# An expert-parallel MoE layer on one core: one late output store and weights in plain order

## The chip, the core and the metric

The kernel runs on one core of one Trainium2 chip. A core has a matrix engine (TensorE, in the profile PE, with its weight loads as PEld), VectorE (DVE), ScalarE (ACT), GpSimd (POOL) and SyncE (SP), an on-chip memory (SBUF) of 128 partitions, and a smaller accumulator memory (PSUM) into which TensorE writes. Sixteen DMA engines move data between the chip's main memory (HBM) and SBUF. They work through queues that SyncE and GpSimd fill. The metric is the device time of one execution in microseconds, as the median of several runs.

## What is computed

Eight experts, each a two-layer network with a ReLU between, on its own 256 rows of input:

```python
n_experts, capacity, hidden, expert_hidden = 8, 256, 512, 2048
x:  (8, 256, 512)    w1: (8, 512, 2048)    w2: (8, 2048, 512)    # all float32

h = np.matmul(x, w1)
h = np.maximum(h, 0)
return np.matmul(h, w2).astype(np.float32)
```

Each w1 and each w2 of an expert is 4 MB in float32, each x and each output 0.5 MB. All of it passes through HBM once: 64 MB of weights, 4 MB of x and 4 MB of output.

## The kernel before

**Loads.** The weights are cast from float32 to bf16 by the DMA itself, so on chip an expert's w1 and w2 are 2 MB each. `load_w1` (line 82) brings a w1 in one DMA. `load_w2` (line 88) brings a w2 in as many DMAs as the table `PIECES` says, counted in sixteenths: one for experts 0 to 5, two halves for expert 6, a half and two quarters for expert 7. `load_x` (line 74) brings the x of two experts at once. All of these are issued by GpSimd, on one queue, and are carried out in the order of issue. The x of experts 0 and 1 alone come through SyncE (line 67) and are cast by VectorE (line 69).

**Order.** The list `loads` holds the loads by expert: x of a pair where one is due, w1, w2. The line `loads[-3], loads[-2] = loads[-2], loads[-3]` exchanges two of them, so that w1 of expert 7 comes ahead of w2 of expert 6. `issue` takes loads from the front of the list as long as they are in the set that it is given, so the main loop says how far ahead loads are issued. There are four buffers for w1 and four for w2; a load waits on GpSimd until the expert that used its buffer has been computed. The order of TensorE's and GpSimd's instructions is the order of the program (`manual_schedule`).

**Compute of one expert.** `prepare` transposes x on TensorE (line 119, 8 transposes) and copies it back to SBUF on VectorE (line 121). `layer1` does 64 matmuls with pieces of w1 as the stationary operand (line 135), and after each 8 of them ScalarE applies the ReLU and writes bf16 (line 142). `layer2` does 32 matmuls (line 161) into two PSUM tiles, one for each half of the 256 rows. Where w2 comes in pieces, both tiles advance together through the pieces; else one tile is finished first. The finished tiles are copied to an output tile in SBUF on VectorE (line 172), the very last one on ScalarE (line 170).

**Main loop.** For each expert from 0 to 6: issue loads, layer 1 of this expert, x of the next one, layer 2 of this expert. In the round of expert 6, layer 1 of expert 7 stands between: TensorE does layer 1 of 6, layer 1 of 7, layer 2 of 6, layer 2 of 7, as the weights arrive in this order.

**Stores.** `GROUPS` sets which outputs share an SBUF tile and a store. Experts 0, 1 and 2 are stored together (1.5 MB, line 92), issued in the round of expert 3; in GpSimd's queue this store stands behind w1 of expert 7 and ahead of w2 of expert 6. Experts 3 to 6 (2 MB, line 92) are stored after everything else on GpSimd. Expert 7's output (0.5 MB, line 174) is stored by SyncE.

The identity matrix for the transposes is built on GpSimd (`make_identity`, a memset and a select), once behind the first and once behind the second weight load.

Of the kernel before, what the change touches and what calls it, by code (L numbers as in the profile page):

```python
# [14 lines left out]
def kernel(  # L15
# [7 lines left out]
    nc = tc.nc  # L23
    P = 128
    E, C, H = x.shape
# [26 lines left out]
    identity = const.tile([P, P], BF16, name="identity")  # L52


    PIECES = {E - 2: [8, 8], E - 1: [8, 4, 4]}


    GROUPS = [(0, 1, 2), (3, 4, 5, 6), (7,)]
    GROUP = {e: g for g in GROUPS for e in g}
    DEFER = GROUPS[-2]  # L60
    X_GROUPS = [(2, 3), (4, 5), (6, 7)]

    xbs, w1s, w2s, outs = {}, {}, {}, {}
# [20 lines left out]
    def load_w2(e):  # L84
        w2s[e] = t = w2_pool.tile([P, K2 * H], BF16, name="w2_sb")
        k = 0
        for n in PIECES.get(e, [K2]):
            nc.gpsimd.dma_start(t[:, k * H:(k + n) * H], w2_v[e, :, k * H:(k + n) * H])  # L88
            k += n

    def store(g):
        nc.gpsimd.dma_start(  # L92
            og_v[:, g[0]:g[-1] + 1, :], outs[g][:].rearrange("p e m h -> p e (m h)")
        )

    loads = []
    for e in range(E):
        for g in X_GROUPS:  # L100
            if g[0] == e + 1:
                loads.append((load_x, g))
        loads += [(load_w1, e), (load_w2, e)]
    loads[-3], loads[-2] = loads[-2], loads[-3]

    def issue(upto):
        while loads:
            f, e = loads[0]
            if (f, e) not in upto:
                break  # L110
            loads.pop(0)
            f(e)

    def prepare(e):
        xb = xbs[e]
        xt_ps = psum_t.tile([P, K1, MC, P], BF16, name="xt_ps")
        for ko in range(K1):
            for mo in range(MC):
                nc.tensor.transpose(xt_ps[:, ko, mo, :], xb[:, mo, :, ko], identity[:])  # L119
        xT = xT_pool.tile([P, K1, C], BF16, name="xT")  # L120
        nc.vector.tensor_copy(  # L121
            xT[:].rearrange("p k c -> p (k c)"),
            xt_ps[:].rearrange("p k m q -> p (k m q)"),
        )
        return xT

    def layer1(e, xT):
        w1_r = w1s[e][:].rearrange("p (ko q j) -> p ko q j", ko=K1, j=K2)
        hT = hT_pool.tile([P, K2, C], BF16, name="hT")
        for pr in range(K2 // 2):  # L130
            h_ps = psum_h.tile([P, 2, C], FP32, name="h_ps")
            for s in range(2):
                j = pr * 2 + s
                for ko in range(K1):
                    nc.tensor.matmul(  # L135
                        h_ps[:, s, :],
                        w1_r[:, ko, :, j],
                        xT[:, ko, :],
                        start=(ko == 0),
                        stop=(ko == K1 - 1),  # L140
                    )
            nc.scalar.activation(  # L142
                hT[:, pr * 2:pr * 2 + 2, :].rearrange("p a c -> p (a c)"),
                h_ps[:].rearrange("p a c -> p (a c)"),
                mybir.ActivationFunctionType.Relu,
            )
        return hT

    def layer2(e, hT):
        last = e == E - 1  # L150
        g = GROUP[e]
        if e == g[0]:
            outs[g] = out_pool.tile([P, len(g), MC, H], FP32, name=f"out_sb{g[0]}")
        out_sb = outs[g][:, e - g[0]]
        o_ps = [psum_o.tile([P, H], FP32, name="o_ps") for _ in range(MC)]
        if e in PIECES:
            order = [(k, m) for k in range(K2) for m in range(MC)]
        else:
            order = [(k, m) for m in range(MC) for k in range(K2)]
        for k, m in order:  # L160
            nc.tensor.matmul(  # L161
                o_ps[m][:],
                hT[:, k, m * P:(m + 1) * P],
                w2s[e][:, k * H:(k + 1) * H],
                start=(k == 0),
                stop=(k == K2 - 1),
            )
            if k == K2 - 1:
                if last and m == 1:
                    nc.scalar.copy(out_sb[:, m, :], o_ps[m][:])  # L170
                else:
                    nc.vector.tensor_copy(out_sb[:, m, :], o_ps[m][:])  # L172
        if last:
            nc.sync.dma_start(out_v[e], out_sb.rearrange("p m h -> p (m h)"))
# [3 lines left out]
    with tc.manual_schedule(engines={mybir.EngineType.PE, mybir.EngineType.Pool}):  # L178
        f, e = loads.pop(0)
        f(e)  # L180
        make_identity(nc, identity)
        f, e = loads.pop(0)
        f(e)
        make_identity(nc, identity)
        issue([(load_w2, 0), (load_x, X_GROUPS[0]), (load_w1, 1), (load_w2, 1), (load_w1, 2)])
        xT = prepare(0)
        for e in range(E - 1):
            issue(
                [(load_w2, e + 2), (load_w1, e + 3), (load_w1, E - 1), (load_w2, e + 1)]
                + [(load_x, g) for g in X_GROUPS if g[0] <= e + 4]  # L190
            )
            for g in GROUPS[:-2]:
                if g[-1] == e - 1:
                    store(g)
            hT = layer1(e, xT)
            xT = prepare(e + 1)
            if e == E - 2:
                hT_last = layer1(E - 1, xT)
            layer2(e, hT)
        store(DEFER)  # L200
        layer2(E - 1, hT_last)
# [1 line left out]
_INS = ['x', 'w1', 'w2']  # L203
_OUTS = [((8, 256, 512), 'float32')]
# [25 lines left out]
```

## Time and profile before

| What | us |
|---|---|
| median of four runs | 182.53 (182.12 to 182.68) |
| the profiled execution: its own time | 182.68 |
| its span, first to last instruction | 180.9 |
| TensorE busy in matmuls | 127.5 |
| ScalarE busy | 40.1 |
| VectorE busy | 17.1 |
| GpSimd busy | 15.4 |

The span is what the profile's views cover; 1.8 us of the profiled time lie outside it. "Idle before" in a group's line is time in which that engine waited, with what ended the wait behind it. TensorE waited 36.4 us at line 135 for w1 and 6.7 us at line 161 for w2; in the last 12 us it waited for nothing. The DMA issues of the page are these; "us to landing" runs from the issue to the arrival of the last byte, the time in the queue included:

```profile
w_sb<-in_w_dram POOLq DMA_DIRECT2D x14, 2048.0 KB, 61.3
w_sb<-in_w_dram POOLq DMA_DIRECT2D x3, 1024.0 KB, 57.4
out_dram<-out_sb POOLq DMA_DIRECT2D x1, 2048.0 KB, 9.8
xb<-in_x_dram POOLq DMA_DIRECT2D x3, 512.0 KB, 45.5
out_dram<-out_sb POOLq DMA_DIRECT2D x1, 1536.0 KB, 64.7
x_sb<-in_x_dram SPq DMA_DIRECT2D x2, 512.0 KB, 3.7
w_sb<-in_w_dram POOLq DMA_DIRECT2D x2, 512.0 KB, 46.8
out_dram<-out_sb SPq DMA_DIRECT2D x1, 512.0 KB, 3.4
```

The sizes are those of the bytes written: a weight of 2048 KB is 4 MB read.

### The profile page before, as it was taken

How to read it: one execution, taken by the hardware profiler on the slowest of the kernel's cores; microseconds unless marked ns; L12 is line 12 of the kernel's file. 1: busy time of each engine (PE TensorE's matmuls, PEld its weight loads, DVE VectorE, ACT ScalarE, POOL GpSimd, SP SyncE). 2: the span in 40 equal slices, each digit the busy share in tenths (PEclk: the TensorE clock that was granted, in tenths of full speed). 3: DMA queues.
4: the chain of work that ended last, by engine and by line, in shares of the span. 5: the costliest groups of instructions: out<-in, count | busy, mean ns of one | idle time of the engine just before them, and what ended most of it. 6: DMA issues, size and time to landing. Idle time of an engine off the chain costs nothing.

```text
span 180.9 us, 1851 instructions
## 1 busy us (share of the span) xinstructions
PE 127.5 (70%) x824; PEld 90.3 (50%) x832; DVE 17.1 (9%) x25; ACT 40.1 (22%) x66; POOL 15.4 (8%) x32
## 2 busy tenths in 40 slices
PE   0206999059994959449994959539994966997780
PEld 0105964048743944138842954228841966953330
DVE  1300011100111011100111011100111010000210
ACT  2001530014400730005500630004600552520000
POOL 7601011010000031000201002010100000000100
PEclk9999999957999999957999999957999998899998
DMA  6998999899999989998999999899989989999994
GB/s 214 250 221 185 232 232 214 192 232 225 206 206 232 225 177 236 232 214 192 232 232 210 196 203 253 185 228 232 221 188 228 232 199 350 226 208 215 219 401 176
DMA packets 4919, 40.48 MB, mean 224 GB/s; under 512 B 432, under 2 KB 432, under 8 KB 2736
## 3 DMA queue, kind: packets, MB, share of 16 engines
q0 software_dynamic: 4480, 38.80, 97.3%
q1 hardware_dynamic: 432, 1.57, 2.4%
q8 instruction: 6, 0.10, 0.2%
q14 instruction: 1, 0.01, 0.0%
HBM read 71.30 MB, written 4.19 MB: 417 GB/s over the span
## 4 chain that ended last, share of the span: by engine, by line
PE 61%; DMA 19%; another core or an unknown queue 15%; POOL 1%; issue 1%; ACT 0%; POOLq 0%
PE h_ps L135 32%; PE o_ps L161 27%; DMA w_sb<-in_w_dram 19%; PE xt_ps L119 1%; POOL xb L74 0%; POOL w_sb L82 0%; ACT out_sb L170 0%; POOL identity masks.py:199 0%; POOL identity masks.py:197 0%; POOL w_sb L88 0%; POOLq masks.py:199 0%; POOLq L214 0%
## 5 line engine op out<-in xcount | busy, mean ns | idle before, releaser
L135 PE MATMUL h_ps<-xT,w_sb 128*128 128x256 bf16 x512 | 67.5, 300 | 36.4 <-DMA w_sb<-in_w_dram 36.4
L135 PEld LDWEIGHTS <-w_sb 128*128 128x128 bf16 x512 | 61.3, 149 | 44.1 <-DMA w_sb<-in_w_dram 39.8
L142 ACT ACTIVATE hT<-h_ps 128x512 bf16<-128x512 f32 x64 | 38.2, 597 | 119.9 <-PE h_ps L135 119.9
L161 PE MATMUL o_ps<-w_sb,hT 128*128 128x512 bf16 x248 | 56.3, 379 | 7.2 <-DMA w_sb<-in_w_dram 6.7
L161 PEld LDWEIGHTS <-hT 128*128 128x128 bf16 x256 | 25.0, 98 | 36.3 <-issue 7.8
L172 DVE COPY out_sb<-o_ps 128x512 f32<-128x512 f32 x15 | 10.3, 691 | 64.4 <-PE o_ps L161 64.4
L121 DVE COPY xT<-xt_ps 128x1024 bf16<-128x1024 bf16 x8 | 5.5, 690 | 90.4 <-PE xt_ps L119 90.4
L88 POOL DMA_DIRECT2D w_sb<-in_w_dram x11 | 5.9, 536 | 57.9 <-DMA w_sb<-in_w_dram 55.6
L119 PE MATMUL xt_ps<-identity,xb 128*128 128x128 bf16 x64 | 5.3, 230 | 4.8 <-DVE xb L69 4.8
L82 POOL DMA_DIRECT2D w_sb<-in_w_dram x8 | 4.7, 593 | 31.7 <-PE h_ps L135 18.6
L119 PEld LDWEIGHTS <-xb 128*128 128x128 bf16 x64 | 4.7, 117 | 4.8 <-DVE xb L69 4.8
L92 POOL DMA_DIRECT2D out_dram<-out_sb x2 | 1.5, 755 | 38.1 <-DVE out_sb L172 37.9
L74 POOL DMA_DIRECT2D xb<-in_x_dram x3 | 2.1, 716 | 26.4 <-PE xt_ps L119 26.4
L170 ACT COPY out_sb<-o_ps 128x512 f32<-128x512 f32 x1 | 0.6, 585 | 15.9 <-PE o_ps L161 15.9
L69 DVE CAST xb<-x_sb 128x1024 bf16<-128x1024 f32 x2 | 1.4, 694 | 4.6 <-DMA x_sb<-in_x_dram 4.6
L142 ACT ACT_TABLE_LOAD x1 | 1.3, 1283 | 0.7 <-PEq L214 0.7
masks.py:199 POOL TENSOR_SCALAR_AFFINE_SELECT identity<-identity 128x128 bf16<-128x128 bf16 x2 | 0.6, 287 | 0.1
masks.py:197 POOL MEMSET identity<- 128x128 bf16 x2 | 0.4, 223 | 0.0
L214 POOL MEMSET const-float32-0.0<- 128x1 f32 x1 | 0.1, 98 | 0.2 <-issue 0.2
L214 POOL MEMSET const-bfloat16-1.0<- 128x1 bf16 x1 | 0.1, 102 | 0.0
L214 POOL MEMSET const-uint8-127<- 128x1 uint8 x1 | 0.1, 102 | 0.0
L214 POOL MEMSET const-float32-1.0<- 128x1 f32 x1 | 0.1, 98 | 0.0
## 6 DMA issues: line engine op xcount, KB each, us to landing
w_sb<-in_w_dram POOLq DMA_DIRECT2D x14, 2048.0 KB, 61.3
w_sb<-in_w_dram POOLq DMA_DIRECT2D x3, 1024.0 KB, 57.4
out_dram<-out_sb POOLq DMA_DIRECT2D x1, 2048.0 KB, 9.8
xb<-in_x_dram POOLq DMA_DIRECT2D x3, 512.0 KB, 45.5
out_dram<-out_sb POOLq DMA_DIRECT2D x1, 1536.0 KB, 64.7
x_sb<-in_x_dram SPq DMA_DIRECT2D x2, 512.0 KB, 3.7
w_sb<-in_w_dram POOLq DMA_DIRECT2D x2, 512.0 KB, 46.8
out_dram<-out_sb SPq DMA_DIRECT2D x1, 512.0 KB, 3.4
```

The lines of the kernel that those rows point to most:

```text
L69: nc.vector.tensor_copy(b[:].rearrange("p m q k -> p (m q k)"), t[:])
L74: nc.gpsimd.dma_start(t[:].rearrange("p e m q k -> p e (m q k)"), xg_v[:, g[0]:g[0] + 2, :])
L82: nc.gpsimd.dma_start(w1s[e][:], w1_v[e])
L88: nc.gpsimd.dma_start(t[:, k * H:(k + n) * H], w2_v[e, :, k * H:(k + n) * H])
L92: nc.gpsimd.dma_start(og_v[:, g[0]:g[-1] + 1, :], outs[g][:].rearrange("p e m h -> p e (m h)"))
L119: nc.tensor.transpose(xt_ps[:, ko, mo, :], xb[:, mo, :, ko], identity[:])
L121: nc.vector.tensor_copy(xT[:].rearrange("p k c -> p (k c)"), xt_ps[:].rearrange("p k m q -> p (k m q)"),)
L135: nc.tensor.matmul(h_ps[:, s, :], w1_r[:, ko, :, j], xT[:, ko, :], start=(ko == 0), stop=(ko == K1 - 1),)
L142: nc.scalar.activation(hT[:, pr * 2:pr * 2 + 2, :].rearrange("p a c -> p (a c)"), h_ps[:].rearrange("p a c -> p (a c)"), mybir.ActivationF ...
L161: nc.tensor.matmul(o_ps[m][:], hT[:, k, m * P:(m + 1) * P], w2s[e][:, k * H:(k + 1) * H], start=(k == 0), stop=(k == K2 - 1),)
L170: nc.scalar.copy(out_sb[:, m, :], o_ps[m][:])
L172: nc.vector.tensor_copy(out_sb[:, m, :], o_ps[m][:])
```

## The change

- Outputs of experts 0 to 6 share one SBUF tile of 28 KB per partition and go out in one store of 3.5 MB, issued on GpSimd behind all loads and behind layer 2 of expert 6. The store in the middle is gone.
- The exchange in the list of loads is gone: w1 of 6, w2 of 6, w1 of 7, w2 of 7. Layer 1 of expert 7 accordingly stands behind layer 2 of expert 6 on TensorE.
- w2 of expert 6 comes in one DMA, w2 of expert 7 in two halves.
- The identity is built once.

```diff
-    PIECES = {E - 2: [8, 8], E - 1: [8, 4, 4]}
+    PIECES = {E - 1: [8, 8]}
...
-    GROUPS = [(0, 1, 2), (3, 4, 5, 6), (7,)]
+    GROUPS = [tuple(range(E - 1)), (E - 1,)]
     GROUP = {e: g for g in GROUPS for e in g}
-    DEFER = GROUPS[-2]
...
-    loads[-3], loads[-2] = loads[-2], loads[-3]
...
         make_identity(nc, identity)
-        f, e = loads.pop(0)
-        f(e)
-        make_identity(nc, identity)
         issue([(load_w2, 0), (load_x, X_GROUPS[0]), (load_w1, 1), (load_w2, 1), (load_w1, 2)])
         xT = prepare(0)
         for e in range(E - 1):
             issue(
-                [(load_w2, e + 2), (load_w1, e + 3), (load_w1, E - 1), (load_w2, e + 1)]
+                [(load_w2, e + 2), (load_w1, e + 3), (load_w2, e + 1)]
                 + [(load_x, g) for g in X_GROUPS if g[0] <= e + 4]
             )
-            for g in GROUPS[:-2]:
-                if g[-1] == e - 1:
-                    store(g)
             hT = layer1(e, xT)
             xT = prepare(e + 1)
-            if e == E - 2:
-                hT_last = layer1(E - 1, xT)
             layer2(e, hT)
-        store(DEFER)
-        layer2(E - 1, hT_last)
+        store(GROUPS[0])
+        hT = layer1(E - 1, xT)
+        layer2(E - 1, hT)
```

## The prediction

> **What bounds the kernel now.** I read first the 40 slices of the page, then the chain that ended last, then the tail in windows and by its DMA issues. All times below are microseconds of the one profiled execution.
>
> ```profile
> PE 127.5 (70%) x824; PEld 90.3 (50%) x832; DVE 17.1 (9%) x25; ACT 40.1 (22%) x66; POOL 15.4 (8%) x32
> ...
> DMA  6998999899999989998999999899989989999994
> ...
> HBM read 71.30 MB, written 4.19 MB: 417 GB/s over the span
> ```
>
> TensorE is busy 70% of the span, the 16 DMA engines nearly all of it, and only the first and last slices are lower. The kernel is one stream of 75.5 MB, and a change helps to the extent that it takes work or a gap out of that stream. The chain of waits shows when each weight became usable, because TensorE waits for it ("another core or an unknown queue" stands where the landing is not attributed):
>
> ```profile
> 38.00 9.52 PE h_ps L135 x64
> ...
> 57.50 7.21 PE h_ps L135 x64
> ...
> 79.32 9.34 PE h_ps L135 x64
> ...
> 98.73 7.21 PE h_ps L135 x64
> ...
> 120.72 9.13 PE h_ps L135 x64
> ...
> 137.43 2.58 another core or an unknown queue
> 140.00 0.05 issue
> 140.05 7.21 PE h_ps L135 x64
> 147.26 0.45 PE xt_ps L119 x8
> 147.71 2.89 another core or an unknown queue
> 150.59 0.05 issue
> 150.64 8.87 PE h_ps L135 x64
> ...
> 164.03 3.61 PE o_ps L161 x16
> ...
> 168.90 4.26 PE o_ps L161 x19
> ```
>
> These are the starts of layer 1 of experts 1 to 7 and of the two waits in layer 2 at the end (second half of w2 of expert 6, first half of w2 of expert 7). From them come the prices of the stream. Two whole weights take 19.50, 19.41 and 19.33 (57.50-38.00, 98.73-79.32, 140.05-120.72), so one takes 9.71. With an x pair between, 21.82 and 21.99, so x is 2.5. A half weight is 4.87 (168.90-164.03). From w1 of expert 7 (150.64) to the end of w2 of expert 6 (164.03) are 13.39; less two halves, 9.74, the 1.5 MB store in the middle of the stream took 3.65, or 2.43 per MB. One step doesn't fit: w1 of expert 7, directly behind w1 of expert 6, took 10.59, which is 0.88 over the 9.71.
>
> ```profile
> out_dram<-out_sb POOLq DMA_DIRECT2D x1, 2048.0 KB, 9.8
> out_dram<-out_sb SPq DMA_DIRECT2D x1, 512.0 KB, 3.4
> ```
>
> These are the two DMA issues of the last 12 (size, time from issue to landing); the next two lines, from the timeline, give their starts.
>
> ```profile
> 169.05 0.76 POOL L92 DMA_DIRECT2D out_dram<-out_sb  x1 [37.93 <-DVE out_sb L172]
> ...
> 176.62 0.35 SPq L174 DMA_DIRECT2D out_dram<-out_sb  x1
> ```
>
> The tail: the 2 MB store lands at 169.05 + 9.8 = 178.85, expert 7's own store at 176.62 + 3.4 = 180.02, and the span is 180.9, so 0.88 follow the last landing. The last weights land near 168.90 + 4.87 = 173.77. The 2.5 MB of output behind them thus end 6.25 later (2.50 per MB, completion included). That is hardly above the 2.43 of the middle store, so the slowest DMA engine has no real gap in the tail, although TensorE computes until 175.98.
>
> **The change part by part.**
> *Middle store gone, one store of 3.5 MB at the end.* Removed: 3.65 ahead of the last w2. Added: 1.5 MB behind it, 3.65 by the same price. Sum 0, unless writes behind each other cost other than writes among reads: 2.43 to 2.50 per MB gives -0.0 to +0.1. The new store holds seven pieces per partition where the old held three and four; both old prices agree, so I scale by bytes. Its cover: it needs expert 6's output. w2 of expert 6 lands at 140.05 + 9.71 = 149.76, its 32 matmuls take 7.07 (the sixth expert's row, 31 matmuls and one before), the copy 0.69: 157.5, and the issue on GpSimd 0.76 for four experts, so up to 1.3 for seven. It stands in the queue from about 158.8, and the weights end at 169.2: 10 of slack. Were that gone, each microsecond of lateness would be one of idle DMA. Nothing is behind this store on GpSimd.
>
> *Plain order of w1 of 7 and w2 of 6.* The bytes are the same. New landings: w2 of 6 at 149.76, w1 of 7 at 159.47, w2 of 7 at 159.47 + 9.74 = 169.21. On GpSimd the three loads now wait for other buffers, but the last five weight transfers are issued 61.6, 60.2, 57.4, 50.4 and 43.2 before they land, so a few microseconds of issue time lie inside the queue.
>
> *Layer 1 of expert 7 moves behind layer 2 of expert 6 on TensorE.* Idle before it: 159.47 - 156.8 = 2.6. In the chain, gaps of 2.58, 2.54 and 2.58 were followed by a layer 1 of 7.21; gaps of 2.93 and about 5 by 8.87 to 9.34. So 7.21 is likely, 9.52 (the longest row) the other end: it ends at 166.7 to 169.0. Layer 2 of expert 7 then is 32 x 0.222 = 7.1 (7.07 in the rows), and its second half of weights is there at 169.21, before its 17th matmul at 170.2. It ends at 173.8 to 176.1, against 175.98 now. The copy (0.58 and 0.03 around it) puts the SP store at 174.4 to 176.7, against 176.62. The 3.5 MB store has bytes left until 169.21 + 3.5 x 2.43 = 177.7, so the SP store joins a busy stream in either case, and the end is set by the stream.
>
> *Pieces.* w2 of 6 comes in one piece instead of two (9.71 against 9.74), w2 of 7 in two instead of three. The quarters have no wait of their own, because TensorE reads them late; their cost is between 0 and what two 512 KB pieces may lose against one of 1 MB, taken as 0.1 from the same kind of difference (0.03) doubled and rounded up. Together -0.03 to -0.13; I take -0.1.
>
> [...]
>
> *Second identity build gone.* Two pairs of instructions, 0.22 + 0.29, ahead of the third DMA issue. That DMA (the x pair) is queued behind eight megabytes of weights, and the first layer 1 waits for w1 at 15.2: 0.
>
> *Sum.* Last weights 169.21, output 4 MB: the 6.25 of the old tail and 1.5 x 2.43 = 3.65 make 9.90, landing 179.1 against 180.02. Of this 0.9, 0.88 is the odd step of w1 of 7, which the sum leaves out because no bytes explain it. If such a delay recurs somewhere in the stream, the gain is the 0.1 of the pieces. The times speak for that: the profiled execution took 182.68, the four runs lie between 182.12 and 182.68, median 182.53, so delays of this size come and go between runs. I take the 0.1 to 0.2 as what is sure, from the median: 182.35.
>
> The clock deserves one more look. [...] The gap of 2.93 before the layer 1 at 150.64 already cost 8.87 - 7.21 = 1.66 here. [...]
>
> **The rivals.**
> *A, bytes conserved (0.45):* the stream is as full as before and carries the same; 182.35, own range 182.1 to 182.7. For it: the tail's 2.50 per MB next to the middle's 2.43. Against it: the odd step.
> *B, the odd 0.88 belongs to the middle store (0.30):* w1 of 7 is the transfer just ahead of that store, and some DMA engines already write output while others still load (the window from 148 to 150 moved 305 GB/s, where weights alone move some 220). Without mixing the step is 9.71, and the end moves by 0.9: 182.53 - 0.9 = 181.65. Against it: nothing like it shows in the tail, where the 2 MB store follows w2 in the same way.
> *C, TensorE becomes the end (0.20), slower:* expert 7's whole compute now hangs on w1 of 7 at 159.47. If that landing is late by the 0.88 (160.35) and the gap so grown (3.5) halves the clock for a while (9.52), layer 2 ends at 160.35 + 9.52 + 7.12 = 177.0, the SP store is issued at 177.6 and lands 3.4 later at 181.0: span 181.9, 0.98 over the old one, time 182.53 + 0.98 = 183.5. It decides from the point at which the last copies end after 176.6. For it: four of the seven quoted layers 1 ran slow. Against: the three at gaps of 2.6 did not.
> *D, the change starves the queue (0.05):* a load waits on GpSimd for a buffer until the queue runs dry; one dry microsecond makes 183.4. Against it: 43 of lead in the least case.
>
> **How the numbers follow.** This kernel's runs tell apart about 0.2%, 0.37 us. A lies almost wholly within it, a little of it on the faster side; B is faster, C and D slower. Faster 0.34, same 0.44, slower 0.22. The range takes in B, with 0.15 below it, and most of C: 181.5 to 183.3; A alone is 182.1 to 182.7.
>
> **What would show it.** In the profile after: no stretch of pure writes before the last weight; layer 1 of expert 7 near 159.5 and 7.2 long; layer 2 of 7 without a wait in its middle; the large store landing about 8.9 after the last weight, and both stores within 1.5 of each other at the end. B shows if w1 of 7 comes 9.7 after w2 of 6 and the span is near 180. C shows as a layer 1 of 9 and an SP store issued after 176.6 that lands last, well after the large one. I am wrong in kind if the output at the end costs clearly more than 2.5 per MB, or if a gap appears in the stream of weights.

## The result, and the profile after

The changed kernel takes 181.89 us (median of 44 runs, 181.50 to 182.55), the kernel before 182.39 us in the same sessions (66 runs, 181.98 to 183.06). The ratio is 0.9973, 95% interval 0.9968 to 0.9979: half a microsecond faster, small and clear of noise.

The profiled execution took 182.45, span 180.7, so it is one of the slower ones of its kernel. Its page, the share of the DMA engines in 40 slices and the issues with size and time to landing:

```profile
DMA  6998999999999989999999999999999999999994
...
HBM read 71.30 MB, written 4.19 MB: 418 GB/s over the span
...
w_sb<-in_w_dram POOLq DMA_DIRECT2D x15, 2048.0 KB, 62.8
out_dram<-out_sb POOLq DMA_DIRECT2D x1, 3584.0 KB, 20.3
...
out_dram<-out_sb SPq DMA_DIRECT2D x1, 512.0 KB, 5.1
```

The same bytes flow as before, and the stream is still full up to the last slice. The chain of waits of the changed kernel from w1 of expert 6 on:

```profile
140.45 0.05 issue
140.49 8.87 PE h_ps L132 x64
149.37 0.45 PE xt_ps L116 x8
149.81 0.32 another core or an unknown queue
150.13 0.04 issue
150.18 0.38 PE o_ps L158
...
157.24 2.61 another core or an unknown queue
159.86 0.05 issue
159.90 7.21 PE h_ps L132 x64
167.11 0.22 PE o_ps L158
167.33 0.05 issue
167.38 6.65 PE o_ps L158 x30
174.03 0.02 issue
174.06 0.58 ACT out_sb L167
```

w2 of expert 6 is usable at 150.13, 9.68 after w1 of 6 (140.45), and w1 of 7 at 159.86, 9.73 later. The step of 10.59 that the old profile had behind w1 of 6 is gone. A w1 of 7 that comes 9.7 after w2 of 6 is the sign that rival B had named. Layer 2 of expert 7 runs without a wait. In the timeline the large store is issued at 158.27, so it lands at 158.27 + 20.3 = 178.6; SyncE's store is issued at 174.66 and lands at 179.8.

Two windows of the same stretch, the kernel before first, then the changed one (columns: stretch, length, busy time of PE, PEld, DVE, ACT and POOL, clock, DMA share, GB/s). A packet is booked where it starts, so a share well above 1 means long packets, or many that start together:

```profile
146.40:147.30 0.90, 0.90 (x12) 0.90 (x11) 0.00 (x0) 0.60 (x2) 0.00 (x0) 1.00 1.78 291
```

```profile
146.40:147.30 0.90, 0.90 (x11) 0.90 (x10) 0.00 (x0) 0.62 (x2) 0.00 (x0) 1.00 1.19 255
```

In the kernel before, 16 packets in a row were slow here, as many as there are DMA engines: 16 KB packets of 1.44 to 2.05 us, where the usual is 1.23, begun between 146.55 and 147.17. The middle store's first packets began at 148.19. In the changed kernel none between 143 and 155 took over 1.23.

The two spans differ by only 0.2, the medians by 0.5. The trace has 16 landings for each transfer, as many as there are DMA engines. For w1 of 6 the first was at 138.47 in the changed kernel's profile and at 138.51 in the old one, but the last at 140.45 and 140.00: up to here both streams carry the same transfers in the same order, and the changed kernel's profile was 0.45 behind. From there to the last landing (179.81 and 180.04) it took 39.36 against 40.04, 0.68 less. Single profiles of this kernel differ by such lags, and a difference of 0.3% is read from the medians.

### The profile page after: what moved, and what is told of

It is laid out like the page before. It is cut to its first block, busy times and chain, and to the rows that moved or that the text cites. A ratio compares the mean times of both kernels' runs of the same rounds, so it can differ in the third digit from the quotient of the medians.

```text
span 180.7 us, 1844 instructions
## 1 busy us (share of the span) xinstructions
PE 126.4 (70%) x824; PEld 89.5 (50%) x832; DVE 17.3 (10%) x25; ACT 40.1 (22%) x66; POOL 13.3 (7%) x27
## 4 chain that ended last, share of the span: by engine, by line
PE 55%; DMA 24%; another core or an unknown queue 14%; POOL 2%; issue 1%; ACT 0%; POOLq 0%
PE o_ps L158 27%; PE h_ps L132 27%; DMA w_sb<-in_w_dram 24%; PE xt_ps L116 1%; POOL w_sb L81 1%; POOL xb L73 0%; ACT out_sb L167 0%; POOL w_sb L87 0%; POOL identity masks.py:199 0%; POOL identity masks.py:197 0%; POOLq masks.py:199 0%; POOLq L204 0%
## 5 line engine op out<-in xcount | busy, mean ns | idle before, releaser
L132 PE MATMUL h_ps<-xT,w_sb 128*128 128x256 bf16 x512 | 66.3, 297 | 36.8 <-DMA w_sb<-in_w_dram 36.8
L132 PEld LDWEIGHTS <-w_sb 128*128 128x128 bf16 x512 | 60.5, 148 | 44.4 <-DMA w_sb<-in_w_dram 40.5
L87 POOL DMA_DIRECT2D w_sb<-in_w_dram x9 | 5.1, 564 | 47.4 <-DMA w_sb<-in_w_dram 47.4
L81 POOL DMA_DIRECT2D w_sb<-in_w_dram x8 | 4.5, 564 | 23.3 <-DMA w_sb<-in_w_dram 18.3
L91 POOL DMA_DIRECT2D out_dram<-out_sb x1 | 1.0, 956 | 48.5 <-DVE out_sb L169 48.5
## 6 DMA issues: line engine op xcount, KB each, us to landing
out_dram<-out_sb POOLq DMA_DIRECT2D x1, 3584.0 KB, 20.3
```

Source lines behind the costliest of these rows:

```text
L81: nc.gpsimd.dma_start(w1s[e][:], w1_v[e])
L91: nc.gpsimd.dma_start(og_v[:, g[0]:g[-1] + 1, :], outs[g][:].rearrange("p e m h -> p e (m h)"))
L132: nc.tensor.matmul(h_ps[:, s, :], w1_r[:, ko, :, j], xT[:, ko, :], start=(ko == 0), stop=(ko == K1 - 1),)
```

## The experiments

Five theories were open: 1, the middle store costs more than its bytes; 2, the pieces of w2; 3, TensorE's earlier end; 4, the order of weights or the second identity build; 5, which came up on the way, GpSimd's closing. All eleven runs have their own runs of the kernel before beside them.

| run | us | ratio to before (95%) |
|---|---|---|
| e1 one store only | 182.73 | 1.0020 (1.0006 to 1.0034) |
| e2 pieces only | 185.86 | 1.0177 (1.0152 to 1.0202) |
| e3 middle store back | 186.03 | 1.0203 (1.0181 to 1.0225) |
| e4 old pieces | 181.94 | 0.9977 (0.9962 to 0.9992) |
| e5 TensorE later | 182.94 | 1.0015 (0.9995 to 1.0035) |
| e6 middle store earlier | 182.96 | 1.0031 (1.0018 to 1.0043) |
| e7 one store, TensorE later | 181.76 | 0.9971 (0.9961 to 0.9980) |
| e8 stores by SyncE | 181.84 | 0.9976 (0.9967 to 0.9984) |
| e9 no middle store | 177.94 | 0.9760 (0.9747 to 0.9772) |
| e10 two identities | 182.00 | 0.9982 (0.9971 to 0.9994) |
| e11 middle store by SyncE | 181.95 | 0.9985 (0.9977 to 0.9994) |

### One part at a time: e1, e2, e3, e4

In the diffs, `...` stands for lines left out. e1, the kernel before with one edit:

```diff
-    GROUPS = [(0, 1, 2), (3, 4, 5, 6), (7,)]
+    GROUPS = [(0, 1, 2, 3, 4, 5, 6), (7,)]
```

> The kernel before with one part of the change alone: outputs 0 to 6 in one late store; order of weights, pieces and both identity builds stay. Theory 1 (the store in the middle costs more than its bytes, because writes are mixed into the weight loads): nearly the whole gain of the change, ratio to before 0.997 to 0.998. Theory 2 (fewer pieces): ratio 1.000. Theory 3 (the end hangs on TensorE and the last 0.5 MB store, and an earlier end of TensorE is the gain): 0.997 to 0.998 too, since w2 of expert 7 lands 3.65 us earlier. Theory 4 (order of weights or the identity build): 1.000.

e2, the kernel before with one edit:

```diff
-    PIECES = {E - 2: [8, 8], E - 1: [8, 4, 4]}
+    PIECES = {E - 1: [8, 8]}
```

> The kernel before with the pieces of the change alone: w2 of expert 6 in one DMA, w2 of expert 7 in two halves. Theory 2: ratio 0.997 to 0.998. Theories 1, 3 and 4, and the prediction's term of 0.03 to 0.13 us: 0.9993 to 0.9998, not to be told from 1.

e3, the changed kernel:

```diff
-    GROUPS = [tuple(range(E - 1)), (E - 1,)]
+    GROUPS = [(0, 1, 2), (3, 4, 5, 6), (7,)]
...
+            if e == 5:
+                store(GROUPS[0])
             issue(
-                [(load_w2, e + 2), (load_w1, e + 3), (load_w2, e + 1)]
+                [(load_w2, e + 2), (load_w1, e + 3 if e < 4 else e + 2), (load_w2, e + 1)]
...
-        store(GROUPS[0])
+        store(GROUPS[1])
```

> The changed kernel with the 1.5 MB store of experts 0 to 2 put back into the middle of the stream, between w2 of 6 and w1 of 7, and a 2 MB store at the end. Theories 1 and 3: the gain is gone, ratio to before 0.999 to 1.000 (theory 3 even if writes cost the same everywhere, since all weights behind the store come 3.65 us later). Theories 2 and 4: 0.997 to 0.998.

e4, the changed kernel:

```diff
-    PIECES = {E - 1: [8, 8]}
+    PIECES = {E - 2: [8, 8], E - 1: [8, 4, 4]}
```

> The changed kernel with the old pieces (w2 of 6 in two halves, w2 of 7 in a half and two quarters). Theories 1, 3, 4: the gain stays, ratio to before 0.997 to 0.998. Theory 2: about 1.000.

No theory foresaw e1, e2 and e3: one store alone (e1), the new pieces alone (e2) and the change with the middle store left in (e3) are all slower than the kernel before. e2 and e3 have one cause, seen in their chains. First e2, then e3:

```profile
163.46 0.59 PE o_ps L161
164.05 0.22 issue
164.27 11.78 PE o_ps L161 x49
176.05 0.05 issue
176.11 2.77 PE o_ps L161 x12
178.87 0.02 issue
```

```profile
159.11 4.91 another core or an unknown queue
164.02 0.05 issue
164.07 8.64 PE h_ps L132 x64
172.71 0.22 PE o_ps L158
172.92 0.05 issue
172.97 6.65 PE o_ps L158 x30
```

In e2 the old order leaves two layers 2 for the end, and with w2 of 6 in one piece neither starts before 163.4: 64 matmuls in a row to 178.9, against 176.0. In e3 w1 of 7 lands behind the middle store, at 164.02, and layer 1 and layer 2 of expert 7 follow it: 179.6. In both TensorE has become the end, and the last store is issued at 179.5 and 180.3. The DMA engines ran dry meanwhile (share of the DMA engines: the last but one number; first e2, whose large store had to wait for layer 2 of 6 and was issued at 172.98, then e3):

```profile
173.00:174.00 1.00, 1.00 (x7) 0.44 (x5) 0.00 (x0) 0.00 (x0) 0.73 (x1) 1.00 0.00 0
```

```profile
179.00:180.00 1.00, 0.61 (x3) 0.10 (x1) 0.57 (x1) 0.35 (x1) 0.00 (x0) 1.00 0.00 0
```

The halves of w2 of 6 were what kept the old order from this, and taking the store out of the middle is what keeps the new order from it. Beside each other the parts are free, as e4 shows: with the new order the pieces make no difference that these runs can tell (181.94 to 181.89).

In e1 the stream is clean: w1 of 7 comes 9.69 after w1 of 6, and TensorE ends at 172.7. Yet it is 0.84 us slower than the changed kernel. Its DMA issues and GpSimd's closing drain (durations in ns, then first and last start) say why:

```profile
out_dram<-out_sb POOLq DMA_DIRECT2D x1, 3584.0 KB, 13.9
out_dram<-out_sb SPq DMA_DIRECT2D x1, 512.0 KB, 6.8
...
L225 POOLq DRAIN  x3: 45/102/14928, 165.9 to 181.3; - x3
```

SyncE's store, issued at 172.67, landed at 179.5; GpSimd's, issued at 165.88, at 179.8. GpSimd's drain, begun at 165.86, ended 14.93 later, at 180.79: 1.0 after its store had landed. The closing barrier waited for it, and the span ended at 181.5, 1.7 after the last landing. In the changed kernel SyncE's store is last, and 0.9 follow it. The profiled execution of e1 took 183.33, 0.6 over its median, so the order of landing is known for that execution alone.

### Who has to end last: e5, e7, e8

e5, the changed kernel with 9 matmuls whose result nobody reads (e7 is e1 with 12 of them at the same place):

```diff
         hT = layer1(E - 1, xT)
+        idle = psum_h.tile([P, 2, C], FP32, name="h_ps")
+        for _ in range(9):
+            nc.tensor.matmul(
+                idle[:].rearrange("p a c -> p (a c)"),
+                hT[:, 0, 0:P],
+                w2s[E - 2][:, 0:H],
+                start=True,
+                stop=True,
+            )
         layer2(E - 1, hT)
```

> The changed kernel with 9 matmuls of no use ahead of layer 2 of expert 7 (2.0 us of TensorE), so that the last 0.5 MB store is issued near 176.7 as in the kernel before, not at 174.66. Theory 3 (the earlier end of TensorE is the gain): the gain goes, ratio to before 0.999 to 1.001. Theory 1 (the middle store disturbed the weight loads, and the end is set by the stream of stores, into which the last store falls in either case): ratio unchanged, 0.997 to 0.998.

> The one-store variant of the kernel before, which was 0.2% slower than it, with 12 matmuls of no use ahead of layer 2 of expert 7, so that SyncE's last store is issued near 174.9 and not at 172.67. Theory 5 (in that variant GpSimd's store landed last, and GpSimd's closing drain ends 1.0 us after its own last store, where SyncE's wait ends at once; so the late landing of GpSimd's store cost 0.65 to 0.85 us): SyncE's store lands last again, and the kernel becomes FASTER by the added work, ratio to before 0.997 to 0.998. Rival (the order w1 of 7 ahead of w2 of 6, or the pieces, costs the 0.8 us): ratio stays 1.002 or rises.

e7 went as theory 5 says: 2.75 us of useless matmuls make the kernel 0.97 us faster than e1 (182.73 to 181.76). Its issues and drain:

```profile
out_dram<-out_sb POOLq DMA_DIRECT2D x1, 3584.0 KB, 12.2
out_dram<-out_sb SPq DMA_DIRECT2D x1, 512.0 KB, 4.7
...
L234 POOLq DRAIN  x3: 45/93/13252, 165.5 to 179.6; - x3
```

GpSimd's store, issued at 165.52, now lands at 177.7, its drain ends at 178.8, and SyncE's store, issued at 174.26, lands last at 179.0. The span is 179.9. Of the 1.6 between the spans of e1 and e7 the closing accounts for 0.8 (1.7 after the last landing in e1, 0.9 here). Why an earlier issue on SyncE turned the order of landing is not shown; that the kernel with the later issue is faster, and by how much, is.

e5 missed its number: 182.94 instead of 181.9. In its profile layer 1 of expert 7 ran 8.88 instead of 7.21, so the last store was issued at 177.64 and not at 176.7:

```profile
159.26 8.88 PE h_ps L132 x64
...
out_dram<-out_sb SPq DMA_DIRECT2D x1, 512.0 KB, 2.7
```

GpSimd's store landed at 177.9, and SyncE's 2.66 after its issue, at 180.3, alone. So e5 passed the point that it was to test. The last landings of the traces decide about theory 3. In the kernel before the last share of the large store landed at 178.81 and that of the last store 1.23 later; in the changed kernel it is 1.24 (178.57 and 179.81), in e7 1.23, in e8 1.25. There the last store followed right behind the large one, and TensorE's end cost nothing. In e5 it is 2.41 (177.89 and 180.30). So TensorE's earlier end isn't the gain, but it is a limit. An estimate of where it begins: 2.66 before the last landings of e7 and of the changed kernel (179.0 and 179.8), an issue between 176.3 and 177.1; for the later stream of the kernel before it is 180.04 - 2.66 = 177.4, past its issue at 176.62. By this estimate the window for SyncE's last issue is some 3 us wide here: 172.7 was too early (e1), 174.1 (e10), 174.66 (the changed kernel) and 176.1 (e8) lie in it, 177.6 was too late.

e8, the changed kernel:

```diff
     def store(g):
-        nc.gpsimd.dma_start(
+        nc.sync.dma_start(
```

> The changed kernel with the 3.5 MB store issued by SyncE and not by GpSimd, at about 158 as before. If an engine finishes GpSimd's queue first (as the last store's packets suggest, which began on each engine when GpSimd's store was through): stores still begin behind w2 of 7, ratio to before 0.996 to 0.998. If the two queues share the engines: the store falls among the last weights, w2 of 7 lands up to 3.65 us later, TensorE ends near 177.4 and the time is 0.5 to 1.5 us over that of the changed kernel, ratio 1.000 to 1.006.

The queues shared the engines: the two halves of w2 of 7 took 5.70 and 6.36 instead of 4.87, and were there at 171.79. The time came out as the other case had it, 181.84: TensorE ended at 176.1, still inside the window, and the bytes are the same.

### What the middle store costs: e6, e9, e11

e6, the kernel before, with the store ahead of the round's loads, so between w1 and w2 of expert 5:

```diff
         for e in range(E - 1):
+            for g in GROUPS[:-2]:
+                if g[-1] == e - 1:
+                    store(g)
             issue(
...
-            for g in GROUPS[:-2]:
-                if g[-1] == e - 1:
-                    store(g)
```

> The kernel before with the middle store two loads earlier in the queue, between w1 and w2 of expert 5. Theory 1: the step of the weight load just ahead of the store becomes the long one (10.1 to 10.7 instead of 9.7 us, now for w1 of expert 5, near 121), the step of w1 of expert 7 becomes 9.7, and the time stays that of before (ratio 0.999 to 1.001). Rival (a delay at a fixed time near 146, whatever stands in the queue): w1 or w2 near 150 stays long and no other step does.

e6's chain around the new place, and at the old one:

```profile
108.11 0.04 issue
...
115.22 6.31 another core or an unknown queue
121.53 0.05 issue
...
144.59 0.05 issue
```

```profile
152.29 2.02 another core or an unknown queue
154.31 0.05 issue
```

From w2 of 4 (108.11) to w1 of 5 (121.53) are 13.42, with an x pair of 2.5 between: 10.9 for the load ahead of the store, where 9.7 is usual. At the old place the step is 9.72 (154.31 - 144.59). Between 116.4 and 118.4, 27 packets of 16 KB took 1.3 to 2.1 us. The delay goes where the store goes, and it doesn't stay at a fixed time: between 143 and 155 no packet took over 1.23 in e6. The time is 0.3% over before, so the place isn't neutral, as theory 1 had expected it to be.

The same step by the landings in the traces, of the last engine and as the mean of the 16:

| load directly ahead of a store in GpSimd's queue, more weights behind | last, us | mean, us |
|---|---|---|
| before, w1 of 7 | 10.59 | 10.17 |
| e2, w1 of 7 | 10.24 | 10.04 |
| e3, w2 of 6 | 10.72 | 10.44 |
| e6, w1 of 5 | 10.94 | 10.45 |
| no store there: after, e1, e5, e7 to e10, and e6 at the old place | 9.68 to 9.72 | 9.70 to 9.72 |

Why a store behind it makes a load slower is not shown by any run.

e9, the kernel before, outputs 0 to 2 never stored:

```diff
-            for g in GROUPS[:-2]:
-                if g[-1] == e - 1:
-                    store(g)
```

> The kernel before without its middle store: outputs 0 to 2 are never written, 1.5 MB fewer in the stream, all else the same. It prices the middle store. Bytes alone (3.65 us): 178.8, ratio to before 0.980. Theory 1 (the store also delays the load ahead of it, by 0.5 to 0.9 us): 177.9 to 178.3, ratio 0.9755 to 0.9775, and no long step for w1 of expert 7.

177.94: the middle store costs 182.33 - 177.94 = 4.39. The same 1.5 MB at the end of the same order (e7) cost 181.76 - 177.94 = 3.82. The difference, 0.57, is the change's gain of 0.50, within what the intervals leave. The trace of the kernel before has the same price: from w1 of 6 to the first half of w2 of 6 the landings lie 18.82 apart in the mean of the 16 engines, and a weight (9.70) and a half (4.86) leave 4.26 for the store. In e6's place it cost 182.96 - 177.94 = 5.02.

e11, the kernel before:

```diff
     def store(g):
-        nc.gpsimd.dma_start(
+        (nc.sync if g[0] == 0 else nc.gpsimd).dma_start(
```

> The kernel before with its middle store issued by SyncE, as soon as experts 0 to 2 are done (near 75), so that it shares the DMA engines with the weight loads instead of standing among them in one queue. If the delay belongs to a store standing in GpSimd's queue ahead of loads: no step is long beyond the store's bytes, ratio 0.997 to 0.998. If any mixing of writes and weight loads costs it: ratio 0.999 to 1.003, and the steps in which the store's packets run are together over 3.65 us longer.

181.95, between the two cases: 4.01 for the store, 0.38 less than on GpSimd's queue among the weights, 0.2 more than at the end, which the intervals hardly tell apart. The trace agrees: the three steps that the store stretches are together 3.98 longer than in the kernel before, in the mean of the engines. So most of the extra cost belongs to the place in GpSimd's queue; sharing the engines with the loads cost about 0.2 (4.01 - 3.82).

### The second identity build: e10

e10, the changed kernel:

```diff
         make_identity(nc, identity)
+        f, e = loads.pop(0)
+        f(e)
+        make_identity(nc, identity)
-        issue([(load_w2, 0), (load_x, X_GROUPS[0]), (load_w1, 1), (load_w2, 1), (load_w1, 2)])
+        issue([(load_x, X_GROUPS[0]), (load_w1, 1), (load_w2, 1), (load_w1, 2)])
```

> The changed kernel with the second identity build back. The prediction priced it at 0: ratio to before as the changed kernel's, 0.997 to 0.998. Theory 4 (the build ahead of the third DMA issue delays the stream): up to 0.5 us more, 0.998 to 1.000.

182.00, ratio 0.9982 with the changed kernel's 0.9973 inside its interval: no cost seen, and up to 0.2 can't be excluded.

## Why the prediction was right, and where not

- *The number.* 181.89 lies in the range of 181.5 to 183.3 because that takes in rival B. The value named, 182.35, and the whole range of rival A, the likeliest, 182.1 to 182.7, lie above it.
- *The bound.* A full stream of DMA, read from the slices and from steps of 9.7: right. Every run that moves all the bytes, has no store among the loads of GpSimd's queue and has TensorE inside its window lies between 181.76 and 182.00.
- *Middle store, sum 0.* This term failed. I priced the middle store from the two landings around it, 3.65, and left the 0.88 in the step ahead of it to chance: "If such a delay recurs somewhere in the stream, the gain is the 0.1 of the pieces. The times speak for that". e9 gives 4.39 in the middle, e7 3.82 at the end, and e6 shows that the delay moves with the store. Rival B was right on whose delay it is; its 0.9 was too much, 0.5 to 0.6 were measured. The wait in the chain overstated it, since it ends with the slowest of 16 engines: in the mean of the engines the step was 10.17, 0.47 over the usual 9.70. B's reason, the mixing of writes and loads, is not shown: in e11 they mix too, and the store costs 4.01.
- *The argument from the spread.* That four runs lie 0.56 apart said nothing about this delay. Kernels without a store in the middle spread as much: the changed one by 1.05 over 44 runs, e7 by 0.74 over 12.
- *Pieces, -0.1.* Not to be told from 0 (e4). e4, with two pieces more than the changed kernel, took 181.94 to its 181.89, 0.05 more. In the old order the pieces are not free: e2 lost 1.8%.
- *Layer 1 of expert 7 behind layer 2 of 6.* Placed rightly: 159.47 foreseen, 159.86 seen; the end of layer 2 at 174.0, in the range of 173.8 to 176.1. The store's issue at 174.66 lies between 174.4 and 176.7. That layer 1 took 7.21 was in part luck: I read it from the gap of 2.6, and e5's profile has 8.88 at the same place behind the same gap.
- *Tail, landing 179.1.* Seen 179.8 in a profile whose slowest engine lagged by 0.45 more than before; 179.0 in e7.
- *Rival C.* It didn't decide. Its threshold, last copies that end after 176.6, agrees with what was seen: e8's ended at 176.1 and kept the gain, e5's at 177.6 and lost it. What I didn't see is the other side of the window, GpSimd's closing.

## What to carry to other kernels

A store that stands in the queue among loads can cost more than its bytes (here 4.39 us there and 3.82 at the end), and here the surcharge was in the transfer ahead of it (10.17 instead of 9.70); look for the one step that is longer than its like, and test it by moving the store, not by asking whether it might be noise. Order, pieces and place of stores formed one balance here between the stream and the tail of compute: one part of a good change taken alone lost 1.8% (e2), and the change without one of its parts 2.0% (e3). At the end of a kernel, look which engine closes last: here it paid to let SyncE, whose wait went on within 0.1 us of the landing where GpSimd's drain took 0.9 to 1.0, have the last transfer (e7 0.97 us under e1).

## What the runs showed of the hardware

- GpSimd's closing drain ended 0.9 to 1.0 us after its last store landed (before, after, e1, e7); SyncE's wait for its own store went on within 0.1 (before, after, e7).
- A gap of 2.6 before a layer 1 didn't settle the clock, as I had read from three rows. By the timeline's idle times, in the changed kernel 2.61 was followed by 8.87 (at 140.49; granted clock 1.00 up to 141.5 and 0.50 from 142.5 to 144.5) and 2.66 by 7.21 (at 159.90; granted clock 1.00); in e5 2.65 by 8.88. So gaps of about 2.6 went both ways, and what told them apart is not shown.
- The page counts instruction fetches among the packets of the 16 DMA engines: six of 16 KB in the kernel before and in the changed one (queue q8 of kind "instruction", 0.2% of the engines' time), 0.9 to 1.0 us each, in the kernel before at 29, 55, 85, 106, 133 and 155. There the engines' landings spread over 0.4 before the first one and over 1.3 after it; the next four changed little (1.5 at w1 of 6), and the step with the middle store brought 2.0. In e1 the spread was 1.2 before any such fetch; whether the fetches have a part in it is not shown. At the end the last engine was 1.3 (e7) to 2.1 (the changed kernel) behind the first with its share of the large store.
